# Weight residues, token sums and the first weight sums around the layer norms move from GpSimd to VectorE, the high copies of the plain slabs from VectorE to ScalarE

## The chip, the cores and the metric

The kernel runs on one core of a Trainium2 chip. The metric is the device time of one launch in microseconds (us), as the median of several runs. The five instruction streams of the core are called PE (TensorE), DVE (VectorE), ACT (ScalarE), POOL (GpSimd) and SP (SyncE, which here only issues DMAs).

## What is computed

An inference step of a two-layer streaming encoder over 576 tokens (512 of a prompt, 64 of a running stream), with D = 1024 and a hidden width of 4096. Layer 0 mixes tokens by chunked band attention, layer 1 by a Mamba-2 scan; each is followed by a dense MLP with squared ReLU. Around all four sublayers stands a post-norm residual. Cut to what matters here:

```python
def _layer_norm(x, g, b):
    mu = mean(x); var = mean(square(x - mu))
    return (x - mu) * rsqrt(var + 1e-5) * g + b

def _mlp(x, w_up, w_down):
    return square(relu(x @ w_up)) @ w_down

for i in range(2):
    m = attention(x) if i % 2 == 0 else ssm(x)
    x = _layer_norm(ALPHA * x + m, ln_mix_g[i], ln_mix_b[i])
    x = _layer_norm(ALPHA * x + _mlp(x, w_ff_up[i], w_ff_down[i]), ln_ff_g[i], ln_ff_b[i])
```

All of it is float32, and the outputs are the new x, the new attention caches and the scan's states.

## The kernel before

**Operands.** Activations lie transposed (features on partitions, tokens along the row) in `x32`, 8 blocks of 128 x 576. Each operand of a matmul is split into a high part (a copy rounded to the matmul's type: `wh` of a weight, `xh` of x, `hh` of a hidden tile, `th` of a sum of tokens) and a low residue, which is the value less that copy (`wl`, `xl`, `hl`, `tl`). A product is three matmuls: high by high, high by low, low by high (`dense`, L313; `dense_half`, L343; `product`, L546).

**Weights.** They come as slabs of 128 x 1024 in the order of `weight_plan`; a raw slab `wr` (four buffers) is loaded by SP, and `Weights.split` makes `wh` on ACT (L188) and `wl` (L189). Split pairs have five buffers, and one is given back when PE has used it (`drop`). L189 runs on DVE, except for the seven slabs around the head of each MLP and of the Mamba input projection (three before that head and four from it on: `pool_lo`, 21 slabs in all), for which it runs on POOL. The matmuls of an MLP's first layer are done in a Strassen form from its seventh slab on; the pair of raw slabs is then first added and subtracted in place in four pieces of 128 x 512 on POOL (L202, L204, L205, L210 in `produce`).

**A layer norm** is a generator that PE's issue loop steps (`side.tick`). It sums x over its blocks (L398 on POOL, in `resid`), has PE average that over the partitions (L406), subtracts (L410, DVE), squares (L413, ACT), adds the squares (L417, L418, DVE), has PE sum them (L367) and forms an inverse root on 96 x 3 values in a row of small DVE instructions (L371, L355, L357, then L360, L361, L362 three times; `y` is the result). PE spreads `y` (L377), DVE multiplies (L428), ACT applies gain and bias (L434), and copies and residues follow (`xh` L439 or L441, `xl` L442 on DVE). The norm is done in halves of 288 tokens. The first half runs beside the last matmuls of the sublayer ahead (`out_last`, the second half of its tokens), the second half beside the first matmuls of the sublayer behind (for an MLP `first_tiles`).

**The first tiles of an MLP.** Six tiles of the first layer are plain. Five of them are made in halves of the tokens (`dense_half`), the first halves beside the norm's second half. `act` then takes a tile out: Relu (L484) and Square (L485) on ACT, the high copy `hh` (L486) on DVE, the residue `hl` (L487) on DVE. Beside the second halves `combos` makes the sums of tokens that the Strassen products need: L502 and L511 on DVE, L506, L514, L515 and L519 on POOL, each with a copy on ACT (L490) and a residue on DVE (L491).

**Order.** Each engine runs its instructions in one fixed order, made when the kernel is built by a scheduler that places all engines' work together. An instruction whose operand isn't there yet holds up all that stand behind it on its engine.

Three stretches of the program are touched: the norm between attention and the first MLP (LN0 below, 300 to 395 us of the span), the norm between that MLP and the Mamba projection (LN1, 725 to 770 us) and the norm between the Mamba layer and the second MLP (LN2, 1240 to 1360 us).

Of the kernel before, what the change touches and what calls it, by code (L numbers as in the profile page):

```python
# [5 lines left out]
F32 = mybir.dt.float32  # L6
# [3 lines left out]
ALU = mybir.AluOpType  # L10
# [31 lines left out]
PLAIN = 6  # L42
DLAG = 5
HALFK = 512
LA = 4
PL0 = -3
PL1 = 4
WARM = 7
HE = 17
DE = 40  # L50
# [34 lines left out]
def weight_plan():  # L85
    plan = []
    for hp in range(8):
        plan += [("q", hp), ("k", hp), ("v", hp)]
    plan += [("wo", c, mp) for c in range(2) for mp in range(4)]

    def mlp(layer):
        p = [("up", layer, 0, m) for m in range(PLAIN)]
        for kind, q, i0, i1 in MLP_ORDER:
            if kind == "up":
                p += [("ups", layer, q, i, g) for i in range(i0, i1) for g in (2, 4, 1, 3)]
            else:
                p += [("down", layer, q, m) for m in range(8)]
        return p

    plan += mlp(0)  # L100
    for g in range(G):
        if g == 0:
            plan += [("dt",), ("c", g), ("b", g), ("x", 2 * g), ("x", 2 * g + 1), ("z", 0), ("z", 1)]
        else:
            plan += [(k, g if k in "cb" else 2 * g + j) for (k, j) in GORD]
        if g in (2, 4):
            plan += [("so", g // 2 - 1, mp) for mp in range(4)]
    plan += [("so", c, mp) for c in (2, 3) for mp in range(4)]
    plan += mlp(1)
    return plan  # L110


def build(nc, io):
    from contextlib import ExitStack
    plan = weight_plan()
    with tile.TileContext(nc) as tc, ExitStack() as es:
        V, S, PE, GP, SY = nc.vector, nc.scalar, nc.tensor, nc.gpsimd, nc.sync
# [9 lines left out]
        def tmp(w=NT):  # L127
            return tp.tile([P, w], F32, name="tmp", tag="tmp")
# [17 lines left out]
        x32 = xp.tile([P, 8, NT], F32, name="x32")  # L146
        xh = xp.tile([P, 8, NT], F32R, name="xh")
        xl = xp.tile([P, 8, NT], F32R, name="xl")

        heads_of = [i for i, p in enumerate(plan) if p[0] in ("up", "c") and p[1:] in ((0, 0, 0), (1, 0, 0), (0,))]  # L150
        pool_lo = {i + j for i in heads_of for j in range(PL0, PL1)}

        class Weights:
            def __init__(self):
                self.done = 0
# [24 lines left out]

            def split(self, i, *raws):
                hi, lo = self.alloc()
                eng = GP if i in pool_lo else V
                c = 0
                for raw in raws:
                    sl = slice(c, c + raw.shape[-1])
                    c = sl.stop
                    S.copy(hi[:, sl], raw)  # L188
                    eng.tensor_tensor(out=lo[:, sl], in0=raw, in1=hi[:, sl].bitcast(F32), op=ALU.subtract)  # L189
                self.t[i] = (hi, lo)  # L190

            def produce(self, i):
                p = plan[i]
                r = self.raw_free
                if p[0] != "ups":
                    self.split(i, self.raw.pop(r))
                    self.raw_free += 1
                    return
                r1, r2 = self.raw[r], self.raw[r + 1]
                lo, hi = slice(0, HALFK), slice(HALFK, 1024)  # L200
                if p[4] == 2:
                    GP.tensor_tensor(out=r2[:, lo], in0=r1[:, lo], in1=r2[:, lo], op=ALU.subtract)  # L202
                    self.split(i, r2)
                    GP.tensor_tensor(out=r2[:, hi], in0=r2[:, hi], in1=r2[:, lo], op=ALU.subtract)  # L204
                    GP.tensor_tensor(out=r2[:, lo], in0=r1[:, lo], in1=r2[:, hi], op=ALU.add)  # L205
                elif p[4] == 4:
                    self.split(i, r2[:, lo])
                elif p[4] == 1:
                    self.split(i, r1)
                    GP.tensor_tensor(out=r1[:, hi], in0=r1[:, hi], in1=r2[:, hi], op=ALU.subtract)  # L210
                else:
                    self.split(i, r2[:, hi], r1[:, hi])
                    del self.raw[r], self.raw[r + 1]
                    self.raw_free += 2
                    self.prefetch()
# [254 lines left out]
        def mlp(layer, ln_in, ln, final):  # L470
            with tc.tile_pool(name=f"mlp{layer}", bufs=1) as hpool:
# [3 lines left out]
                T1, T2 = slice(0, HALF), slice(HALF, NT)  # L475
# [5 lines left out]
                def act(src, q, m, t0, t1):  # L481
                    u, t = tmp(), tmp()
                    hh, hl = (x[:, m % 2, t0:t1] for x in H[q, m // 2])
                    S.activation(u[:, t0:t1], src, AF.Relu)  # L484
                    S.activation(t[:, t0:t1], u[:, t0:t1], AF.Square)  # L485
                    V.tensor_copy(hh, t[:, t0:t1])  # L486
                    V.tensor_tensor(out=hl, in0=t[:, t0:t1], in1=hh.bitcast(F32), op=ALU.subtract)  # L487

                def combine(dh, dl, t):
                    S.copy(dh, t)  # L490
                    V.tensor_tensor(out=dl, in0=t, in1=dh.bitcast(F32), op=ALU.subtract)  # L491

                def sums_of(kk):
                    t = tmp().rearrange("p (a b) -> p a b", a=2)
                    return t, slice(2 * kk, 2 * kk + 2), slice(4 + 2 * kk, 6 + 2 * kk)

                def combos():
                    k1, k2 = slice(0, 4), slice(4, 8)
                    for kk in range(2):
                        o = slice(2 * kk, 2 * kk + 2)  # L500
                        t, j1, j2 = sums_of(kk)
                        V.tensor_tensor(out=t, in0=x32[:, j2, T2], in1=x32[:, j1, T2], op=ALU.subtract)  # L502
                        combine(th[:, o, :], tl[:, o, :], t)
                        yield
                    t2 = collect()
                    GP.tensor_tensor(out=t2, in0=x32[:, k2, T2], in1=x32[:, k1, T2], op=ALU.subtract)  # L506
                    yield
                    for kk in range(2):
                        o1, o4 = slice(4 + 2 * kk, 6 + 2 * kk), slice(8 + 2 * kk, 10 + 2 * kk)
                        t, j1, j2 = sums_of(kk)  # L510
                        V.tensor_tensor(out=t, in0=x32[:, j1, T2], in1=x32[:, j1, T1], op=ALU.subtract)  # L511
                        combine(th[:, o1, :], tl[:, o1, :], t)
                        yield
                        GP.tensor_tensor(out=t, in0=t, in1=x32[:, j2, T2], op=ALU.subtract)  # L514
                        GP.tensor_tensor(out=t, in0=t, in1=x32[:, j2, T1], op=ALU.add)  # L515
                        yield
                        combine(th[:, o4, :], tl[:, o4, :], t)
                        yield
                    GP.tensor_tensor(out=t2, in0=t2, in1=x32[:, k1, T1], op=ALU.add)  # L519
                    last.append(t2)  # L520

                last = []
# [1 line left out]
                def collect():  # L524
                    return hpool.tile([P, 4, HALF], F32, name="ut", tag="ut", bufs=2)
# [361 lines left out]
        def ssm():  # L887
            cumd = dr.tile([32, NT], F32, name="cumd")
            expd = dr.tile([32, NT], F32, name="expd")
            with tc.tile_pool(name="ssm", bufs=2) as ap:  # L890
# [156 lines left out]
                def ssd(g, c, b, x0, x1, z0, z1):  # L1047
# [120 lines left out]
                    if g < 6:  # L1168
                        split(g, yy)
                    else:  # L1170
                        ys[g] = yy
# [20 lines left out]
                for g in (6, 7):  # L1192
                    split(g, ys[g])
# [79 lines left out]
def make(A):  # L1273
    import concourse.bacc as bacc
    nc = bacc.Bacc("TRN2", target_bir_lowering=False, num_devices=1)
    io = {}
    for k, a in A.items():
        io[k] = nc.dram_tensor("in_" + k, a.shape, F32, kind="ExternalInput").ap()
    for k, s in OUTS.items():
        io[k] = nc.dram_tensor("out_" + k, s, F32, kind="ExternalOutput").ap()  # L1280
    build(nc, io)
    return nc
# [20 lines left out]
```

## Time and profile before

| | before |
|---|---|
| median of 3 runs | 1732.73 us (1728.52 to 1733.08) |
| the profiled execution | 1731.92 us |
| its span | 1730.1 us |
| mean granted clock of PE | 0.981 of full speed |
| busy: PE, DVE, ACT, POOL | 1667.4, 1085.2, 767.3, 460.0 us |
| share of the chain that ended last: PE, DVE, ACT, POOL | 87%, 7%, 2%, 1% |

The span is the profiled execution from its first to its last instruction; some 1.8 us of the execution's time lie around it. Busy time is the sum over an engine's instructions, and two engines can be busy at once. The chain of work that ended last is followed back from the last instruction; an engine's share in it is the time that this engine's work, or what it waited for, sets directly. A granted clock below 1 means that in some stretches PE was run at the lower of its two speeds.

### The profile page before, as it was taken

The page shows a single profiled execution, that of the slowest core. Times are in us where ns is not written, and L with a number is a line of the kernel's source. Part 1 is how long each engine was busy: PE and PEld are TensorE (multiplying, and loading weights), DVE is VectorE, ACT ScalarE, POOL GpSimd, SP SyncE. Part 2 cuts the span into 40 slices and gives each one's busy share as a digit, 9 for nine tenths or more (in the row PEclk, how much of TensorE's full clock was granted, in tenths as well). Part 3 has the DMA queues.
Part 4 walks back from the last instruction along what each step waited for, and adds up shares of the span by engine and source line. Part 5 has one row for each costly group of instructions (what it writes and reads, how often), then busy time and mean ns, then how long its engine had stood idle before and what let it go on. Part 6 is the DMA issues. An engine that isn't in the chain of part 4 may idle for free.

```text
span 1730.1 us, 30824 instructions
## 1 busy us (share of the span) xinstructions
PE 1667.4 (96%) x12545; PEld 1591.5 (92%) x12545; DVE 1085.2 (63%) x1860; ACT 767.3 (44%) x1256; POOL 460.0 (27%) x453
## 2 busy tenths in 40 slices
PE   9999999889999999989999999999988999999995
PEld 8888887779999999989899999999978999999995
DVE  6555565795363736377876776777768836455446
ACT  5434442445261625245663563565225616254332
POOL 0000001441221212336541341344343313131211
PEclk9999999989999999999999999999998999999998
DMA  8343331103141323213332332333210312223121
GB/s 267 104 127 102 109 110 65 61 20 127 38 136 58 103 69 118 66 61 120 116 107 83 99 107 87 95 107 101 66 61 25 110 55 93 86 74 122 50 74 55
DMA packets 76925, 157.22 MB, mean 91 GB/s; under 512 B 11440, under 2 KB 40240, under 8 KB 76784
## 3 DMA queue, kind: packets, MB, share of 16 engines
q1 hardware_dynamic: 76784, 155.25, 27.7%
q8 instruction: 99, 1.62, 0.4%
q14 instruction: 42, 0.34, 0.1%
HBM read 145.80 MB, written 9.42 MB: 90 GB/s over the span
## 4 chain that ended last, share of the span: by engine, by line
PE 87%; DVE 7%; ACT 2%; POOL 1%; issue 1%; DMA 0%; SPq 0%; POOLq 0%; DVEq 0%; ACTq 0%
PE mm L313 54%; PE ax L546 12%; PE mm L546 5%; PE mm L343 2%; PE ax L802 2%; PE mm L322 1%; PE ax L824 1%; PE ax L1107 1%; PE ax L773 1%; PE ax L1110 1%; DVE tmp L417 1%; PE ax L377 1%; PE ax L1112 1%; PE ax L783 1%; PE ax L367 1%
## 5 line engine op out<-in xcount | busy, mean ns | idle before, releaser
L188 ACT CAST wh<-wr 128x1024 fp32r<-128x1024 f32 (+1 forms) x301 | 281.6, 938 | 476.4 <-PE mm L313 351.1
L189 DVE TENSOR_TENSOR wl<-wr,wh 128x1024 fp32r<-128x1024 f32 (+1 forms) x280 | 332.1, 1189 | 103.1 <-ACT wh L188 97.6
L313 PE MATMUL mm<-xh,wh 128*128 128x288 f32 x1088 | 239.9, 302 | 7.1 <-ACT tmp L484 7.0
L313 PE MATMUL mm<-xh,wl 128*128 128x288 f32 x1088 | 239.7, 301 | 0.0
L313 PE MATMUL mm<-xl,wh 128*128 128x288 f32 x1088 | 239.5, 301 | 0.0
L313 PE MATMUL mm<-hh,wl 128*128 128x288 f32 x960 | 223.4, 298 | 0.0
L313 PE MATMUL mm<-hh,wh 128*128 128x288 f32 x960 | 223.1, 298 | 0.0
L313 PE MATMUL mm<-hl,wh 128*128 128x288 f32 x960 | 222.9, 297 | 0.0
L389 DVE TENSOR_TENSOR x<-x,mm 128x288 f32<-128x288 f32 (+1 forms) x112 | 64.7, 581 | 206.8 <-PE mm L313 195.8
L313 PEld LDWEIGHTS mm<-xh,wh 128*128 128x128 f32 x1088 | 176.6, 191 | 9.9 <-ACT tmp L484 7.4
L313 PEld LDWEIGHTS mm<-xl,wh 128*128 128x128 f32 x1088 | 176.3, 191 | 4.1 <-issue 3.8
L313 PEld LDWEIGHTS mm<-xh,wl 128*128 128x128 f32 x1088 | 176.2, 190 | 1.5
L313 PEld LDWEIGHTS mm<-hh,wl 128*128 128x128 f32 x960 | 161.3, 190 | 0.1
L313 PEld LDWEIGHTS mm<-hl,wh 128*128 128x128 f32 x960 | 161.4, 190 | 0.0
L313 PEld LDWEIGHTS mm<-hh,wh 128*128 128x128 f32 x960 | 161.2, 190 | 0.1
L546 PE MATMUL ax<-xh,wh 128*128 128x288 f32 x416 | 122.9, 295 | 0.4 <-ACT ut L564 0.4
L546 PE MATMUL ax<-xl,wh 128*128 128x288 f32 x416 | 122.6, 295 | 0.0
L546 PE MATMUL ax<-xh,wl 128*128 128x288 f32 x416 | 122.5, 294 | 0.0
L202 POOL TENSOR_TENSOR wr<-wr 128x512 f32<-128x512 f32 x26 | 35.7, 1374 | 271.5 <-DMA wr<-in_wts 271.4
L918 DVE SCALAR_TENSOR_TENSOR tmp<-xpad,pm,tmp 128x579 f32<-128x579 f32 x90 | 88.9, 987 | 1.6 <-ACT tmp L916 0.8
L343 PE MATMUL mm<-xl,wh 128*128 128x288 f32 x240 | 74.3, 310 | 8.1 <-DVE xl L442 8.0
L546 PEld LDWEIGHTS ax<-xh,wh 128*128 128x128 f32 x416 | 78.1, 188 | 1.3 <-ACT ut L564 1.3
(264 smaller groups left out, 3643.0 us busy)
## 6 DMA issues: line engine op xcount, KB each, us to landing
wr<-in_wts SPq DMA_DIRECT2D x223, 512.0 KB, 3.4
cumb<-cumd SPq DMA_DIRECT2D x32, 256.0 KB, 3.7
e<-expd SPq DMA_DIRECT2D x48, 64.0 KB, 3.5
tb<-in_rel SPq DMA_DIRECT2D x16, 160.0 KB, 3.0
out_k<-tmp SPq DMA_DIRECT2D x8, 288.0 KB, 2.4
out_v<-tmp SPq DMA_DIRECT2D x8, 288.0 KB, 2.1
tb<-in_rel SPq DMA_DIRECT2D x16, 144.0 KB, 2.9
ts<-in_rel SPq DMA_DIRECT2D x16, 144.0 KB, 3.1
```

Source lines behind the costliest of these rows:

```text
L188: S.copy(hi[:, sl], raw)
L189: eng.tensor_tensor(out=lo[:, sl], in0=raw, in1=hi[:, sl].bitcast(F32), op=ALU.subtract)
L202: GP.tensor_tensor(out=r2[:, lo], in0=r1[:, lo], in1=r2[:, lo], op=ALU.subtract)
L313: PE.matmul(ps[:, o:o + HALF], w, a(k)[:, t0:t0 + HALF], start=first and i == 0, stop=last and i == 2)
L322: PE.matmul(ps[:, PS0 + t0:PS0 + t0 + HALF], w, a(k)[:, t0:t0 + HALF], start=k == 0 and i == 0, stop=k == 7 and i == 2)
L343: PE.matmul(o, a, b[:, k, h * HALF:(h + 1) * HALF], start=k == 0 and i == 0, stop=k == 7 and i == 2)
L367: PE.matmul(ps[0:96, j:j + 1], vv[:, 96 * j:96 * j + 96], scale_col, start=True, stop=True)
L377: PE.matmul(ps[:, 96 * j:96 * j + 96], y[:, j0 + j:j0 + j + 1].to_broadcast([96, 128]), ident[0:96, 0:96], start=True, stop=True)
L389: V.tensor_tensor(out=dst, in0=dst, in1=src, op=ALU.add)
L546: chain(PE.matmul(out, a, b, start=not more and k == 0 and i == 0, stop=k == 3 and i == 2, skip_group_check=True), k or i or name != "t3")
L802: PE.transpose(pp[:, 128 * k:128 * k + 128], s[:, 128 * k:128 * k + 128], ident)
L918: V.scalar_tensor_tensor(out=acc, in0=xr[:, k:k + 579], scalar=col(k), in1=acc, op0=ALU.mult, op1=ALU.add)
```

## The change

All L189 residues run on DVE, and the table `pool_lo` goes. In `combos` the four kinds of POOL sums (L506, L514, L515, L519) run on DVE. The four weight sums of the first Strassen pair of each MLP run on DVE, those of all other pairs stay on POOL. The high copies `hh` of the plain tiles (L486) run on ACT. The sums L398 of the norms stay on POOL.

Counted over the program, DVE gets from POOL 21 residues of 128 x 1024, 4 token sums of 128 x 1152, 8 token sums of 128 x 576 and 8 weight sums of 128 x 512; ACT gets from DVE 22 copies, 20 of 128 x 288 and 2 of 128 x 576.

```diff
@@ class Weights, split
-                eng = GP if i in pool_lo else V
...
                     S.copy(hi[:, sl], raw)
-                    eng.tensor_tensor(out=lo[:, sl], in0=raw, in1=hi[:, sl].bitcast(F32), op=ALU.subtract)
+                    V.tensor_tensor(out=lo[:, sl], in0=raw, in1=hi[:, sl].bitcast(F32), op=ALU.subtract)
@@ class Weights, produce
+                eng = V if p[2:4] == (0, PLAIN // 2) else GP
                 if p[4] == 2:
-                    GP.tensor_tensor(out=r2[:, lo], in0=r1[:, lo], in1=r2[:, lo], op=ALU.subtract)
+                    eng.tensor_tensor(out=r2[:, lo], in0=r1[:, lo], in1=r2[:, lo], op=ALU.subtract)
...
@@ mlp, act
-                    V.tensor_copy(hh, t[:, t0:t1])
+                    S.copy(hh, t[:, t0:t1])
                     V.tensor_tensor(out=hl, in0=t[:, t0:t1], in1=hh.bitcast(F32), op=ALU.subtract)
@@ mlp, combos
-                    GP.tensor_tensor(out=t2, in0=x32[:, k2, T2], in1=x32[:, k1, T2], op=ALU.subtract)
+                    V.tensor_tensor(out=t2, in0=x32[:, k2, T2], in1=x32[:, k1, T2], op=ALU.subtract)
...
-                        GP.tensor_tensor(out=t, in0=t, in1=x32[:, j2, T2], op=ALU.subtract)
-                        GP.tensor_tensor(out=t, in0=t, in1=x32[:, j2, T1], op=ALU.add)
+                        V.tensor_tensor(out=t, in0=t, in1=x32[:, j2, T2], op=ALU.subtract)
+                        V.tensor_tensor(out=t, in0=t, in1=x32[:, j2, T1], op=ALU.add)
...
-                    GP.tensor_tensor(out=t2, in0=t2, in1=x32[:, k1, T1], op=ALU.add)
+                    V.tensor_tensor(out=t2, in0=t2, in1=x32[:, k1, T1], op=ALU.add)
```

Line numbers in the changed kernel are lower by 5 to 6 behind `split` (L355 there is the first product of a root step, L360 of the kernel before), and the scheduler makes a new order on every engine. Two places of DVE's order in LN0 show it. The first is the inverse root of the norm's first half, from the row that takes PE's sums (`v`) to the one before the multiplication of x. Before:

```order
L371 TENSOR_SCALAR v<-ax_3897 96x3
L355 TENSOR_SCALAR w<-v 96x3
L357 TENSOR_SCALAR y<-w 96x3
L360 TENSOR_TENSOR w<-y 96x3
L361 SCALAR_TENSOR_TENSOR w<-w,v 96x3
L362 SCALAR_TENSOR_TENSOR y<-w,y 96x3
L360 TENSOR_TENSOR w<-y 96x3
L389 TENSOR_TENSOR x_78<-x_78,mm 128x288
L361 SCALAR_TENSOR_TENSOR w<-w,v 96x3
```

The same place in the changed kernel:

```order
L366 TENSOR_SCALAR v<-ax_3897 96x3
L183 TENSOR_TENSOR wl<-wr,wh 128x1024
L350 TENSOR_SCALAR w<-v 96x3
L384 TENSOR_TENSOR x_78<-x_78,mm 128x288
L352 TENSOR_SCALAR y<-w 96x3
L355 TENSOR_TENSOR w<-y 96x3
L183 TENSOR_TENSOR wl<-wr,wh 128x1024
L356 SCALAR_TENSOR_TENSOR w<-w,v 96x3
L384 TENSOR_TENSOR x_78<-x_78,mm 128x288
L357 SCALAR_TENSOR_TENSOR y<-w,y 96x3
```

Two residues of weights (L183 there) now stand inside the row of small instructions, a third stands just ahead of it among the sums of squares, and a fourth right behind it.

The second place is the end of the norm's second half, where the last residues `xl` of x are made beside the sums of tokens. Before:

```order
L442 TENSOR_TENSOR xl<-x_78,xh 128x2x288
L502 TENSOR_TENSOR tmp<-x_78 128x576
L442 TENSOR_TENSOR xl<-x_78,xh 128x2x288
L486 CAST hh<-tmp 128x288
L491 TENSOR_TENSOR tl<-tmp,th 128x576
```

In the changed kernel, where L501 and L514 are the two sums of 128 x 1152 that were L506 and L519 on POOL:

```order
L437 TENSOR_TENSOR xl<-x_78,xh 128x2x288
L501 TENSOR_TENSOR ut<-x_78 128x1152
L437 TENSOR_TENSOR xl<-x_78,xh 128x2x288
L482 TENSOR_TENSOR hl<-tmp,hh 128x288
L497 TENSOR_TENSOR tmp<-x_78 128x576 x2
L506 TENSOR_TENSOR tmp<-x_78 128x576
L486 TENSOR_TENSOR tl<-tmp,th 128x576
L514 TENSOR_TENSOR ut<-ut,x_78 128x1152
```

One of those sums now stands ahead of the last `xl`, in the place of a smaller one, and the copy `hh` is gone from between them.

## Rows read from the trace of the kernel before

**Rows 1.** Waits of PE in LN0: line waited for, us in total, times, longest.

```profile
PE mm L343 <- DVE xl L442: 3.9, 1, 3.9
PE ax L377 <- DVE y L362: 3.8, 1, 3.8
PE mm L313 <- ACT tmp L484: 3.8, 1, 3.8
PE ax L367 <- ACT tmp L485: 1.8, 1, 1.8
```

**Rows 2.** Waits of PE in LN1.

```profile
PE ax L367 <- DVE tmp L418: 3.0, 2, 2.3
...
PE ax L406 <- POOL tmp L398: 0.5, 1, 0.5
```

**Rows 3.** Waits of PE in LN2.

```profile
PE ax L377 <- DVE y L362: 4.3, 2, 3.8
PE mm L343 <- DVE xl L442: 4.1, 2, 4.0
PE mm L313 <- ACT tmp L484: 3.2, 1, 3.2
PE mm L313 <- DVE yl L1179: 1.8, 1, 1.8
```

**Rows 4.** Busy us (x count) of PE, PEld, DVE, ACT, POOL; clock; DMA share, GB/s.

```profile
300.00:395.00 95.00, 79.21 (x530) 76.94 (x529) 79.62 (x115) 41.62 (x72) 44.93 (x30) 0.89 0.13 45
412.00:464.00 52.00, 52.00 (x392) 52.00 (x391) 16.69 (x20) 12.04 (x13) 6.48 (x5) 1.00 0.22 75
```

**Rows 5.** The same view: nine stretches at the lower clock; the last line is their sum.

```profile
324.90:331.70 6.80, 5.89 (x25) 5.90 (x26) 4.96 (x10) 3.47 (x7) 2.17 (x3) 0.50 0.25 77
...
1263.50:1266.90 3.40, 3.40 (x16) 3.40 (x16) 0.91 (x2) 0.00 (x0) 0.80 (x1) 0.50 0.48 154
...
sum 51.20, PE 44.27 PEld 43.01 DVE 43.39 ACT 28.30 POOL 21.15; mean PE 4.92 PEld 4.78 DVE 4.82 ACT 3.14 POOL 2.35
```

**Rows 6.** Timeline of DVE in LN0: start, us, line, operation [idle before].

```profile
312.64 2.47 DVE L417 TENSOR_TENSOR tmp<-tmp 128x576 f32<-128x576 f32 x1
...
315.40 0.75 DVE L417 TENSOR_TENSOR tmp<-tmp 128x576 f32<-128x576 f32 x1
...
317.22 0.94 DVE L418 TENSOR_TENSOR tmp<-tmp 128x288 f32<-128x288 f32 x1
...
323.30 2.26 DVE L361 SCALAR_TENSOR_TENSOR w<-w,v 96x3 f32<-96x3 f32 x1
325.59 0.16 DVE L362 SCALAR_TENSOR_TENSOR y<-w,y 96x3 f32<-96x3 f32 x1
...
330.74 0.75 DVE L442 TENSOR_TENSOR xl<-x,xh 128x576 fp32r<-128x576 f32 x1
...
357.82 3.23 DVE L502 TENSOR_TENSOR tmp<-x 128x576 f32<-128x576 f32 x1
360.98 3.16 DVE L442 TENSOR_TENSOR xl<-x,xh 128x576 fp32r<-128x576 f32 x1
```

**Rows 7.** Timeline of POOL in LN0.

```profile
312.10 2.40 POOL L189 TENSOR_TENSOR wl<-wr,wh 128x1024 fp32r<-128x1024 f32 x1 [3.43 <-ACT wh L188]
...
323.20 2.34 POOL L189 TENSOR_TENSOR wl<-wr,wh 128x1024 fp32r<-128x1024 f32 x1
...
357.72 2.71 POOL L506 TENSOR_TENSOR ut<-x 128x1152 f32<-128x1152 f32 x1 [13.91 <-ACT x L434]
360.51 3.02 POOL L519 TENSOR_TENSOR ut<-ut,x 128x1152 f32<-128x1152 f32 x1
```

**Rows 8.** Timeline of ACT in LN0.

```profile
376.97 1.56 ACT L188 CAST wh<-wr 128x512 fp32r<-128x512 f32 x2 [2.24 <-POOL wr L205]
379.33 0.67 ACT L490 CAST th<-tmp 128x576 fp32r<-128x576 f32 x1 [0.79 <-DVE tmp L511]
```

**Rows 9.** The page's costliest groups: DVE's residues of weights (busy us, mean ns).

```profile
L189 DVE TENSOR_TENSOR wl<-wr,wh 128x1024 fp32r<-128x1024 f32 (+1 forms) x280 | 332.1, 1189 | 103.1 <-ACT wh L188 97.6
```

More of the change, by code (lines that the diff above doesn't have):

```diff
@@ L45 @@
 LA = 4
-PL0 = -3
-PL1 = 4
 WARM = 7
@@ L148, in build @@
         xl = xp.tile([P, 8, NT], F32R, name="xl")
-        heads_of = [i for i, p in enumerate(plan) if p[0] in ("up", "c") and p[1:] in ((0, 0, 0), (1, 0, 0), (0,))]
-        pool_lo = {i + j for i in heads_of for j in range(PL0, PL1)}
         class Weights:
@@ L200, in produce @@
                 lo, hi = slice(0, HALFK), slice(HALFK, 1024)
+                eng = V if p[2:4] == (0, PLAIN // 2) else GP
                 if p[4] == 2:
-                    GP.tensor_tensor(out=r2[:, lo], in0=r1[:, lo], in1=r2[:, lo], op=ALU.subtract)
+                    eng.tensor_tensor(out=r2[:, lo], in0=r1[:, lo], in1=r2[:, lo], op=ALU.subtract)
                     self.split(i, r2)
-                    GP.tensor_tensor(out=r2[:, hi], in0=r2[:, hi], in1=r2[:, lo], op=ALU.subtract)
-                    GP.tensor_tensor(out=r2[:, lo], in0=r1[:, lo], in1=r2[:, hi], op=ALU.add)
+                    eng.tensor_tensor(out=r2[:, hi], in0=r2[:, hi], in1=r2[:, lo], op=ALU.subtract)
+                    eng.tensor_tensor(out=r2[:, lo], in0=r1[:, lo], in1=r2[:, hi], op=ALU.add)
                 elif p[4] == 4:
@@ L209, in produce @@
                     self.split(i, r1)
-                    GP.tensor_tensor(out=r1[:, hi], in0=r1[:, hi], in1=r2[:, hi], op=ALU.subtract)
+                    eng.tensor_tensor(out=r1[:, hi], in0=r1[:, hi], in1=r2[:, hi], op=ALU.subtract)
                 else:
```

## The prediction

> **What bounds the kernel.** I read the waits of PE first, stretch by stretch. Away from the norms there is nothing to win: in 52 us of a down stage PE is busy for 52.00 us at full clock [rows 4]. In LN0 eight waits sum to 15.8 us, three of them of nearly 4 us [rows 1]; in LN1 three sum to 5.7 [rows 2]; in LN2 ten sum to 17.9 [rows 3]. Together PE stands still for 39.4 us. The busy table adds a second loss: the 95 us of LN0 ran at a mean granted clock of 0.89 [rows 4], and nine stretches in or right behind these waits show 0.50, that is 1.2 instead of 2.4 GHz [rows 5].
>
> What ends the waits is DVE for the most part, so DVE's timeline comes next, with POOL's beside it. The sum L417 took 2.47 us at 312.64 and 0.75 us three microseconds later; the 96 x 3 product L361 took 2.26 us at 323.30, where its neighbour of the same size took 0.16; L502 and L442, both of 128 x 576, took 3.23 and 3.16 us, where another L442 cost 0.75 at 330.74 [rows 6]. Each of these four lies beside a long POOL instruction that began 0.1 to 0.5 us before it: residues at 312.10 and 323.20, token sums at 357.72 and 360.51 [rows 7]. Each of the four ends 0.6 us behind the POOL row, or with it for the small one: POOL's end, and then its own work. So DVE waits inside its instruction until POOL is done, and the excess of the four is 1.7 + 2.1 + 2.5 + 2.4 = 8.7 us. The second of them lies inside the chain to `y`, for which PE waits 3.8 us; the last is the `xl` for which PE waits 3.9 us [rows 1].
>
> The Trainium skill, "SBUF — State Buffer", section on SBUF's two separate sides, says that a DVE operation with two operands in SBUF and a GpSimd operation exclude each other for the whole instruction. The four rows agree; that some may be late for another reason is a rival below.
>
> **The change, part by part.** *Work that moves.* At 1.19 us for a residue [rows 9] and 0.75 us for a two-operand 128 x 576 [rows 6], scaled with the size for the others (an estimate), DVE gets 21 x 1.19 = 25.0, 8 x 0.75 = 6.0, 4 x 1.50 = 6.0 and 8 x 0.67 = 5.3 us: 42.3 us, of which LN0 and LN2 get 17.0 each and LN1 8.3. From this go the 22 copies of `hh`, which I don't count.
>
> *What goes.* With the moved work POOL has in these stretches little left but the sums L398 and the later Strassen pairs. If the lengthening goes, so do the waits that it makes. In LN0:
> - `y`. DVE begins the first L417 at 312.64 as before. From there to the end of L418 the changed order has three L417, one L418, two evictions and one residue: 3 x 0.75 + 3 x 0.45 + 1.19, less some 0.08 for each by which rows overlap, 4.3 us: 316.9, against 318.2 now [rows 6]. Behind it come PE's sums (0.9 us with the hop) and, up to `y`, two residues, three evictions and twelve small rows: 2.4 + 1.1 + 12 x 0.19 = 5.8 us. So `y` is there at 323.6, against 325.75. PE has about 38 matmuls, 5 us, to do meanwhile, so the wait of 3.8 us becomes about 0.5.
> - PE now reaches the first plain tile at about 326.9. The first `xl` began 5.0 us behind `y` [rows 6] and takes 0.75, with a wait of 0.5 for an eviction between them that falls away: 328.8. **A new wait of 1.9 us** stands there; before, the long wait for `y` hid it.
> - The second half: the L485 wait of 1.8 us goes, because its Square stood behind late sums (L417) in the queues. The `xl` wait of 3.9 goes; the sum ahead of the last `xl` costs 1.3 to 1.5 us where the two long rows together cost 6.4.
> - The 3.8 us for L484 is ACT's queue: the Relu stands behind copies that waited for L205 on POOL and for L511 on DVE [rows 8]. Both come early when POOL's row of sums is gone. I keep 0.3.
> - Kept: three small waits, for L418, L389 and L387, with 1.9 together. With 0.5, 1.9 and 0.3 from above: 4.6 us of waits are left of 15.8.
>
> *The lower clock.* At full clock 392 matmuls take 52.00 us, 0.133 each [rows 4]. The nine stretches hold 186 matmuls (25 in the first) in 44.27 us of busy time [rows 5], so they cost 44.27 - 186 x 0.133 = 19.6 us more than at full clock: 7.2 in LN0 (67 matmuls in three stretches), 2.6 in LN1 (30 in two), 9.8 in LN2 (89 in four). The Trainium skill, "TensorE: Matmul & The Clock Gate", section Terms, prices a lowered clock at the whole lowered time by the lost share of pulses; by that rule it would be 51.2 / 2 = 25.6 us. The rows decide for 19.6, since PE idles in part of those stretches. A wait as short as the 1.8 us for L1179 [rows 3] was followed by 3.4 us at the lower clock, which cost 3.40 - 16 x 0.133 = 1.3 us [rows 5]; I charge that for each wait of 1.9 us or more that is left.
>
> *The sum.*
> - LN0: at most 15.8 + 7.2 = 23.0 us. Left: 4.6 + 1.3 = 5.9. Gain 17.1.
> - LN1: at most 5.7 + 2.6 = 8.3. Seven residues on DVE ahead of the first `xh` leave a wait of about 2.3, as long as the longest now [rows 2], with 1.3 of clock, and L406 keeps its 0.5 (POOL's L398 stays). Gain 4.2.
> - LN2: at most 17.9 + 9.8 = 27.7. The four waits of rows 3 go, 13.4 us (L1179's residue stood beside one on POOL). Left: 4.5, the new 1.9, 1.3 of clock. Gain 20.0.
>
> Together 41.3 us from the profiled 1731.92: 1690.6, and since the median lies 0.8 above that execution, **1691 us**. What had no row before is the copy `hh` on ACT: at most 0.67 us, a copy of twice the size [rows 8], 22 times 14.7 us in two stretches where ACT is busy for 42 of 95 us [rows 4]; it costs nothing at best (ACT idles beside it), and at worst keeps the waits for L484. I take nothing, since Relu, Square and copy now follow each other without a hop to DVE and back. A price that the four rows can't exclude is that of DVE's own two-operand work against the remaining L398: 0.5 to 2 us.
>
> **The rivals.**
> 1. *ACT's queue keeps PE waiting.* The copies make ACT's queue longer by up to 7 us a stretch, and it also holds Square, gain and bias, `xh` and `wh`. Then the 3.8 and 3.2 us for L484 stay [rows 1, 3], with the lower clock behind them (2.4 and 2.8 us, of the shares of LN0 and LN2 above): 12.2 us less gain, 1703. For: ACT ends 8.8 us of these waits already. Against: ACT waited there for POOL and DVE, not the other way round [rows 8].
> 2. *Residues hold up the roots.* Those among the small rows wait for `wh` from ACT, as the first residue on POOL did for part of 3.43 us [rows 7], and `wh` waits for PE to free a buffer. On POOL that held up nobody; on DVE the whole chain to `y` stands behind it. Then the waits for `y` stay at 3.8 in LN0 and LN2, with about 2.6 of clock each: 2 x (3.3 + 2.6) = 11.8 less, 1703. Both rivals together: 1715.
> 3. *Slower: DVE is full.* DVE is busy 79.6 of 95 us in LN0 [rows 4]. If its long rows are long for a reason of its own and not POOL's, 17.0 us are added to 15.4 idle ones, and the idle ones are waits for PE that can't be filled. Then the added 42.3 us push the chain directly: up to 1774, or, with half hidden, 1753. It decides as soon as the rows of 2 to 3 us don't shrink. For: the share; the changed order puts residues into the chain. Against: the L417 at 315.40 and the L442 at 330.74, with no long POOL row beside them, took 0.75 [rows 6]. The Trainium skill, "Perfetto Trace Analysis", section Optimizing Scalar/DVE Operations, advises to offload a saturated DVE, even to GPSIMD, with the reservation that the two share a port: the first half speaks against this change, and by it 1753 would be the time; the rows above go with the reservation.
> 4. *The waits were set elsewhere,* by PE's own order or by loads, and the change only renames them: 1732.
>
> **How the numbers follow.** The forecast as summed, within 10 us for the terms that a walk by hand misses (hops of 0.1 to 0.2 us between engines, a lower clock behind one wait more or less): 0.66. Rivals 1 or 2: 0.22, both at once included. More than the sum, to the floor of 1673 at which no wait and no lower clock is left: 0.03. No change: 0.05; slower: 0.04. The range from 1679 to 1712 holds the first and all of the second but its far end. What a measurement can tell from no change is 0.3%, 5.2 us: faster 0.91, within 0.05, slower 0.04.
>
> **What would show it.** Right: DVE's L417, L361, L502 and L442 rows (five lines lower in the changed code) take 0.75, 0.16, 0.75, 0.75 us everywhere in these stretches; the waits for `y` are under 1 us, that for `xl` is gone, a new one of about 2 us stands ahead of the first plain tile; PE's clock shows 0.50 in at most one short stretch for each norm; DVE's busy time rises by less than the 42 us, because what it no longer waits for is in that count too. Wrong in size: PE waits for L484 or `y` as long as before, with ACT or a `wh` copy ahead of it. Wrong in mechanism: DVE's rows stay at 2 to 3 us with POOL idle beside them.

## The result and the profile after

The changed kernel takes 1702.03 us (median of 4 runs, 1701.69 to 1706.24) against 1731.3 us before (4 runs): a ratio of 0.9838 with an interval of 0.9816 to 0.9860, so 24 to 32 us faster. The forecast of 1691 overstated the gain: 41 us were forecast, 30.2 came (spans 1730.1 and 1699.9 of the profiled executions). The range held it, but 1702 lies 11 us above the sum, outside the 10 us that the forecast gave to the sum itself. Two executions, one of e5 at 4016 us and one of the kernel before beside it at 2737 us, lie far off all others and are left out of the times and ratios below.

The page of the changed kernel, busy time of each engine:

```profile
PE 1652.7 (97%) x12545; PEld 1576.5 (93%) x12545; DVE 1064.4 (63%) x1879; ACT 774.8 (46%) x1278; POOL 378.1 (22%) x412
```

Two things stand in this line. PE's busy time fell by 14.7 us with the same 12545 matmuls: that is the lower clock. The other 15.5 us of the 30.2 are time in which PE stood still. And DVE's busy time fell by 20.8 us (1085.2 before) although it was given 41 instructions of POOL's, some 42 us of work by the prediction's prices, less the 22 copies (12.6 us before): what went is time in which its instructions stood still.

The busy table of three stretches that hold the norms in the changed kernel (busy us and count of PE, PEld, DVE, ACT, POOL, then the granted clock) answers to [rows 4]:

```profile
300.00:380.00 80.00, 74.72 (x538) 72.35 (x538) 67.21 (x118) 45.82 (x84) 17.21 (x14) 0.98 0.13 42
705.00:755.00 50.00, 45.10 (x322) 43.41 (x321) 36.15 (x70) 21.01 (x34) 8.38 (x16) 0.97 0.17 56
1225.00:1325.00 100.00, 90.98 (x668) 88.37 (x666) 79.33 (x145) 48.22 (x87) 21.44 (x17) 0.97 0.13 44
```

The clock of LN0 went from 0.89 in its 95 us to 0.98 in these 80. Of the nine stretches at the lower clock in and behind the norms [rows 5] three are left, one for each norm, 13.7 us where there were 51.2:

```profile
332.40:335.80 3.40, 3.40 (x14) 3.10 (x13) 2.59 (x4) 2.16 (x5) 1.09 (x1) 0.50 0.00 0
735.10:738.50 3.40, 3.29 (x12) 3.00 (x13) 3.40 (x5) 3.37 (x6) 0.06 (x1) 0.50 0.36 107
1277.80:1284.70 6.90, 3.87 (x15) 3.44 (x15) 6.78 (x11) 5.99 (x12) 0.00 (x0) 0.51 0.22 78
```

PE's waits in LN0, LN1 and LN2, one below the other, answer to [rows 1 to 3]:

```profile
PE mm L338 <- DVE x L384: 2.2, 1, 2.2
PE ax L372 <- DVE y L357: 1.1, 1, 1.1
PE mm L338 <- ACT tmp L479: 0.9, 1, 0.9
PE mm L308 <- DVE x L384: 0.7, 2, 0.4
PE mm L308 <- DVE x L382: 0.3, 1, 0.3
...
PE mm L338 <- DVE xh L434: 2.5, 1, 2.5
PE ax L362 <- DVE tmp L413: 0.9, 1, 0.9
PE ax L401 <- POOL tmp L393: 0.9, 1, 0.9
...
PE ax L401 <- POOL tmp L393: 2.7, 1, 2.7
PE mm L338 <- DVE xh L434: 2.5, 1, 2.5
PE mm L308 <- DVE x L384: 2.2, 3, 1.5
PE mm L541 <- ACT ut L552: 1.5, 1, 1.5
```

The three waits for `y`, `xl` and L484 that took 11.5 us in LN0 are 1.1, none and none; the 0.9 for L479 stands ahead of a half tile, where PE waited 0.7 for L484 before. New is the wait of 2.2 to 2.5 us ahead of the first plain tile (L338 for L384 or for `xh`), in every norm; and one that the prediction doesn't have, L541 for L552, in the Strassen products behind LN2 and, outside this window at 390 us, behind LN0.

How much each norm gave is read from PE landmarks: the first instruction of LN1's averages (L406, now L401), before and after, and the same statistics row of the Mamba stage (L367, now L362), before and after. The view is that of one source line in a window, with first and last start:

```profile
L406 PE MATMUL ax<-tmp,invd x2: 405/405/405, 726.6 to 726.9; 128*128 128x288 f32 x2
```

```profile
L401 PE MATMUL ax<-tmp,invd x2: 405/405/405, 713.1 to 713.4; 128*128 128x288 f32 x2
```

```profile
L367 PE MATMUL ax<-inv,tmp x12: 166/223/223, 1028.9 to 1029.8; 128*96 128x1 f32 x12
```

```profile
L362 PE MATMUL ax<-inv,tmp x12: 166/223/223, 1014.5 to 1015.4; 128*96 128x1 f32 x12
```

LN0 gave 726.6 - 713.1 = 13.5 us (17.1 forecast), LN1 14.4 - 13.5 = 0.9 (4.2 forecast), LN2 the rest, 30.2 - 14.4 = 15.8 (20.0 forecast).

DVE's timeline of LN0 in the changed kernel shows a part of why it was less than the walk by hand had it:

```profile
313.40 0.76 DVE L412 TENSOR_TENSOR tmp<-tmp 128x576 f32<-128x576 f32 x1
...
315.11 1.22 DVE L183 TENSOR_TENSOR wl<-wr,wh 128x1024 fp32r<-128x1024 f32 x1
...
318.64 1.71 DVE L183 TENSOR_TENSOR wl<-wr,wh 128x1024 fp32r<-128x1024 f32 x1
...
320.98 1.84 DVE L183 TENSOR_TENSOR wl<-wr,wh 128x1024 fp32r<-128x1024 f32 x1
...
323.55 0.67 DVE L356 SCALAR_TENSOR_TENSOR w<-w,v 96x3 f32<-96x3 f32 x1
...
325.07 0.65 DVE L357 SCALAR_TENSOR_TENSOR y<-w,y 96x3 f32<-96x3 f32 x1
```

The L412 rows take 0.76 us, as forecast. But the two residues inside the root take 1.71 and 1.84 instead of 1.22, and two of the 96 x 3 rows 0.67 and 0.65 instead of 0.16: 2.1 us in all. Beside each of them POOL runs one of the norm's sums, L393:

```profile
318.47 0.80 POOL L393 TENSOR_TENSOR tmp<-tmp,x 128x288 f32<-128x288 f32 x1
320.93 0.81 POOL L393 TENSOR_TENSOR tmp<-tmp,x 128x288 f32<-128x288 f32 x1 [1.66 <-DVE y L352]
323.39 0.81 POOL L393 TENSOR_TENSOR tmp<-tmp,x 128x288 f32<-128x288 f32 x1 [1.66 <-DVE y L357]
324.92 0.79 POOL L393 TENSOR_TENSOR tmp<-tmp,x 128x288 f32<-128x288 f32 x1 [0.72 <-DVE w L355]
...
367.18 5.95 POOL L197 TENSOR_TENSOR wr<-wr 128x512 f32<-128x512 f32 x1 [33.68 <-DMA wr<-in_wts]
```

The last row is the other way round: the first weight sum of the second Strassen pair, 1.30 us in the median of 24 such rows, stood on POOL for 5.95 us while DVE ran one two-operand row after the other. The wait of L541 comes from the second pair's sums on POOL, as e6 below shows; that this one row is what made them late is read from the rows and not tested.

So `y` is ready at 325.72 us, as late as before (325.75). Counted from PE's average it comes after 16.0 us instead of 16.8; in LN1 after 16.2 instead of 16.5, in LN2 after 17.1 instead of 17.5. The residues' own time and L393 take nearly all that the short rows give back. PE's wait for `y` fell all the same, because in the new order PE does more of the sublayer's matmuls (L308, before L313) between the average and the spread of `y`: 90 instead of 70 in LN0, 101 and 82 instead of 70 in LN1 and LN2. The busy table from the average to the spread in LN0, before and after:

```profile
308.93:325.81 16.88, 11.25 (x81) 10.23 (x79) 15.74 (x27) 5.45 (x7) 9.99 (x6) 0.97 0.17 63
309.69:325.78 16.09, 13.98 (x101) 12.93 (x99) 15.13 (x32) 6.50 (x8) 4.09 (x5) 1.00 0.29 99
```

PE is busy 2.7 us longer there, in a stretch that is 0.8 us shorter. The chain to the last `xl` of the second half did get shorter: from PE's average to the end of that row 28.1 us before and 23.2 after.

### The profile page after: what moved, and what is told of

The parts are those of the page before. It is cut to its first block, busy times and chain, and to the rows that moved or that the text cites. A ratio compares the mean times of both kernels' runs of the same rounds, so it can differ in the third digit from the quotient of the medians.

```text
span 1699.9 us, 30804 instructions
## 1 busy us (share of the span) xinstructions
PE 1652.7 (97%) x12545; PEld 1576.5 (93%) x12545; DVE 1064.4 (63%) x1879; ACT 774.8 (46%) x1278; POOL 378.1 (22%) x412
## 5 line engine op out<-in xcount | busy, mean ns | idle before, releaser
L183 DVE TENSOR_TENSOR wl<-wr,wh 128x1024 fp32r<-128x1024 f32 (+1 forms) x301 | 359.9, 1200 | 106.1 <-ACT wh L182 100.9
L308 PE MATMUL mm<-xh,wl 128*128 128x288 f32 x1088 | 237.8, 299 | 0.0
L308 PE MATMUL mm<-xh,wh 128*128 128x288 f32 x1088 | 237.5, 300 | 0.1
L308 PE MATMUL mm<-xl,wh 128*128 128x288 f32 x1088 | 237.4, 299 | 0.0
L308 PE MATMUL mm<-hh,wl 128*128 128x288 f32 x960 | 222.0, 297 | 0.0
L308 PE MATMUL mm<-hl,wh 128*128 128x288 f32 x960 | 221.7, 296 | 0.0
L308 PE MATMUL mm<-hh,wh 128*128 128x288 f32 x960 | 221.7, 296 | 0.0
L384 DVE TENSOR_TENSOR x<-x,mm 128x288 f32<-128x288 f32 (+1 forms) x112 | 64.5, 580 | 196.2 <-PE mm L308 185.1
L308 PEld LDWEIGHTS mm<-xl,wh 128*128 128x128 f32 x1088 | 174.3, 189 | 4.1 <-issue 3.8
L308 PEld LDWEIGHTS mm<-xh,wh 128*128 128x128 f32 x1088 | 174.5, 188 | 2.6 <-issue 1.4
L308 PEld LDWEIGHTS mm<-xh,wl 128*128 128x128 f32 x1088 | 174.3, 189 | 1.5
L308 PEld LDWEIGHTS mm<-hh,wl 128*128 128x128 f32 x960 | 160.1, 188 | 0.1
L308 PEld LDWEIGHTS mm<-hh,wh 128*128 128x128 f32 x960 | 160.1, 188 | 0.1
L308 PEld LDWEIGHTS mm<-hl,wh 128*128 128x128 f32 x960 | 160.1, 188 | 0.0
L541 PE MATMUL ax<-xh,wh 128*128 128x288 f32 x416 | 123.1, 296 | 0.5 <-ACT ut L559 0.4
L541 PE MATMUL ax<-xl,wh 128*128 128x288 f32 x416 | 122.6, 295 | 0.0
L541 PE MATMUL ax<-xh,wl 128*128 128x288 f32 x416 | 122.5, 294 | 0.0
L197 POOL TENSOR_TENSOR wr<-wr 128x512 f32<-128x512 f32 x24 | 40.7, 1695 | 337.9 <-DMA wr<-in_wts 297.8
L338 PE MATMUL mm<-xh,wh 128*128 128x288 f32 x240 | 72.8, 307 | 8.3 <-DVE xh L434 5.1
L541 PEld LDWEIGHTS ax<-xh,wh 128*128 128x128 f32 x416 | 78.1, 188 | 1.6 <-ACT ut L559 1.3
```

Of the source, the lines that this page charges most:

```text
L183: V.tensor_tensor(out=lo[:, sl], in0=raw, in1=hi[:, sl].bitcast(F32), op=ALU.subtract)
L197: eng.tensor_tensor(out=r2[:, lo], in0=r1[:, lo], in1=r2[:, lo], op=ALU.subtract)
L308: PE.matmul(ps[:, o:o + HALF], w, a(k)[:, t0:t0 + HALF], start=first and i == 0, stop=last and i == 2)
L338: PE.matmul(o, a, b[:, k, h * HALF:(h + 1) * HALF], start=k == 0 and i == 0, stop=k == 7 and i == 2)
L384: V.tensor_tensor(out=dst, in0=dst, in1=src, op=ALU.add)
L541: chain(PE.matmul(out, a, b, start=not more and k == 0 and i == 0, stop=k == 3 and i == 2, skip_group_check=True), k or i or name != "t3")
```

## The experiments

Theory A: a two-operand row of DVE stands still while a POOL row runs, and those made the waits. Theory B: DVE is full, and more work on it costs time. Others stand with the runs. Each time is a median; the ratio is to the kernel before on the same chip.

| run | what | us | ratio, 95% |
|---|---|---|---|
| e1 | residues alone | 1721.73 | 0.9946 (0.9929 to 0.9964) |
| e2 | token and first weight sums alone | 1715.64 | 0.9908 (0.9884 to 0.9932) |
| e3 | copies `hh` alone | 1727.91 | 0.9979 (0.9968 to 0.9990) |
| e4 | the change without the residues | 1715.57 | 0.9902 (0.9875 to 0.9930) |
| e8 | the change with an idle twin of each residue on POOL | 1726.42 | 0.9971 (0.9957 to 0.9985) |
| e9 | the same with a twin of 128 x 8 | 1703.68 | 0.9832 (0.9818 to 0.9847) |
| e5 | the change, norm sums on DVE too | 1701.63 | 0.9821 (0.9796 to 0.9847) |
| e6 | the change, second pair's sums on DVE too | 1698.95 | 0.9813 (0.9792 to 0.9835) |
| e7 | e5 and e6 together | 1695.63 | 0.9795 (0.9772 to 0.9818) |
| e10 | e7, first `xh` on ACT | 1698.24 | 0.9797 (0.9782 to 0.9811) |
| e11 | e7, LN1's residues on POOL | 1696.68 | 0.9796 (0.9776 to 0.9815) |

**The parts alone.** e1 is the kernel before with

```diff
-                eng = GP if i in pool_lo else V
+                eng = V
```

> Kernel before with one part of the change: all 21 weight residues on VectorE; token sums, first weight sums and hh copies stay where they were. Theory A (VectorE's two-operand rows stand still while a GpSimd row runs, and that made the waits): L417 and L361 beside the norms fall to 0.75 and 0.2 us, the wait for y falls below 1.5 us in LN0 and LN2, the xl wait (3.9) and the L484 wait (3.8) stay; about 1717 us, 14 less than before. Theory B (VectorE is full, more work on it costs): the residues stand in the chain to y; not faster than before, 1731 or more.

It took 10.8 us less than before. In LN0 the wait for `y` is 1.1, those for `xl` and L484 stay:

```profile
PE mm L343 <- DVE xl L442: 4.1, 2, 4.0
PE mm L313 <- ACT tmp L484: 3.2, 1, 3.2
PE mm L343 <- DVE x L389: 2.2, 1, 2.2
PE ax L377 <- DVE y L362: 1.1, 1, 1.1
```

L417 fell to 0.76 us and L361 to between 0.15 and 0.67, as theory A has it, and 25 us more work on DVE made the kernel faster, against B. But `y` comes 16.0 us behind PE's average, as in the whole change, and PE has its 90 matmuls before the spread here too. A kernel with the residues on POOL and PE's later spread was not run, so how much of this gain is the order's and how much the short rows' isn't shown. The expectation left out the wait of 2.2 us ahead of the first plain tile, which is here as in the whole change; the gain is 3 us smaller than expected.

e2 moves the other POOL rows:

```diff
-                    GP.tensor_tensor(out=t2, in0=x32[:, k2, T2], in1=x32[:, k1, T2], op=ALU.subtract)
+                    V.tensor_tensor(out=t2, in0=x32[:, k2, T2], in1=x32[:, k1, T2], op=ALU.subtract)
...
+                eng = V if p[2:4] == (0, PLAIN // 2) else GP
```

> Kernel before with another part: token sums and the first pair's weight sums on VectorE; residues stay on GpSimd, hh copies on VectorE. Theory A: the xl wait (3.9 and 4.0) and the L484 wait (3.8 and 3.2) go with the lower clock behind them, the wait for y (3.8 and 3.8) stays; about 1714 us, 17 less than before. Theory B: 17 us of added VectorE work in LN0 and LN2 end up in front of the first Strassen products; 1731 or more.

It took 16.9 us less; in LN0 the wait for `y` is 3.8 as before, `xl` is gone, and a wait of 2.4 us for a weight residue (L189) stands where L484 stood. The last `xl` ends 22.9 us behind the average instead of 28.1. Theory A again, and here the chain itself is shorter.

e3 moves the copies alone:

```diff
-                    V.tensor_copy(hh, t[:, t0:t1])
+                    S.copy(hh, t[:, t0:t1])
```

> Kernel before with the last part alone: the 22 copies hh on ScalarE. Theory A: no wait is removed, since none of them was made by these copies; within 3 us of before (1728 to 1734). Theory C (the copies' hop between ScalarE and VectorE is what kept PE waiting for L484): the two L484 waits go, 10 us or more less than before, 1721.

It took 4.6 us less, a little more than theory A allowed by the medians (the interval, 0.9968 to 0.9990, allows 2 to 6 us). Theory C falls: the L484 wait didn't go but grew, in LN2 from 3.2 to 6.0 too. Theory A's "no wait is removed" isn't borne out either, for `xl` fell from 3.9 to 1.0. The waits of LN0 sum to 15.4 us, as good as before (15.8); what was won is for the most part the lower clock, since PE's busy time fell by 5.8 us to 1661.6:

```profile
PE mm L313 <- ACT tmp L484: 6.0, 1, 6.0
PE ax L377 <- DVE y L362: 3.8, 1, 3.8
PE ax L367 <- DVE tmp L418: 2.5, 2, 1.9
PE mm L343 <- DVE xl L442: 1.0, 1, 1.0
```

The three parts add up to 32 us, the whole change gave 29 by the medians: little of one is hidden by another. e4 is the check from the other side, the change with `pool_lo` kept.

> Changed kernel with the 21 weight residues back on GpSimd. Theory A: the gain splits by place, so this loses what the residues alone won: waits for y of 2 us or more in LN0 and LN2 and in LN1 as before; about 1716, 14 more than the changed kernel. Theory B: the residues on VectorE cost something, so taking them off gives 1702 or less.

It lost 13.5 us by the medians and 11 by the ratios, with the wait for `y` at 3.8 us in LN0, 3.5 in LN1 and 2.3 in LN2, about what theory A expected. PE is back at 70 matmuls before the spread, so this run doesn't part the order from the short rows either.

**The lock by itself.** These runs keep all the work of the change on DVE and ACT, and give POOL rows on which nothing depends but the raw slab's release:

```diff
+                if i in pool_lo:
+                    GP.tensor_tensor(out=raws[0], in0=raws[0], in1=hi.bitcast(F32), op=ALU.subtract)
                 self.t[i] = (hi, lo)
```

> Changed kernel, with GpSimd computing each of the 21 residues a second time, behind VectorE's own, into the raw slab that nobody reads any more. No result depends on it; VectorE and ScalarE have the work of the changed kernel. Theory A: VectorE's rows beside these twins take 2 to 3 us again (L412, L356, L437), the waits for y come back to 2 us or more; 1712 to 1722 us, 10 to 20 more than the changed kernel. Theory D (what counted was that nobody waits for GpSimd's results any more, not the lock): 1702 within 3.

It took 1726.42 us: 24 of the 29 us are lost again, more than the 10 to 20 of theory A. DVE's rows in LN0 (line numbers are those of the kernel before, the twin is L188):

```profile
316.90 2.24 DVE L418 TENSOR_TENSOR tmp<-tmp 128x288 f32<-128x288 f32 x1
...
322.78 0.45 DVE L389 TENSOR_TENSOR x<-x,mm 128x288 f32<-128x288 f32 x1 [0.95 <-PE mm L313]
323.15 1.09 DVE L357 TENSOR_SCALAR y<-w 96x3 int32<-96x3 int32 x1
...
326.48 2.13 DVE L362 SCALAR_TENSOR_TENSOR y<-w,y 96x3 f32<-96x3 f32 x1
```

and POOL's twins beside them:

```profile
316.08 2.74 POOL L188 TENSOR_TENSOR wr<-wr,wh 128x1024 f32<-128x1024 f32 x1 [7.03 <-ACT wh L185]
...
321.83 2.39 POOL L188 TENSOR_TENSOR wr<-wr,wh 128x1024 f32<-128x1024 f32 x1 [1.16 <-DVE w L355]
...
326.20 2.38 POOL L188 TENSOR_TENSOR wr<-wr,wh 128x1024 f32<-128x1024 f32 x1 [1.23 <-DVE w L361]
```

L418 takes 2.24 us instead of 0.45 and ends 0.32 behind the twin (318.82); the root's L362 takes 2.13 instead of 0.16 and ends with its twin (328.6). PE waits 2.7 us for `y` in LN0 and 4.8 in LN1; in LN2 it doesn't, the time lost there stands in other waits. DVE's busy time is 1082.6 us, 18 more than in the changed kernel, for the same DVE work.

The control shrinks the twin and keeps its waits, what it releases and its place in the program:

```diff
-                    GP.tensor_tensor(out=raws[0], in0=raws[0], in1=hi.bitcast(F32), op=ALU.subtract)
+                    GP.tensor_tensor(out=raws[0][:, 0:8], in0=raws[0][:, 0:8], in1=hi[:, 0:8].bitcast(F32), op=ALU.subtract)
```

> As the twin before (the changed kernel with a second residue on GpSimd that nobody reads), but of 128 x 8 elements instead of 128 x 1024: the same 21 instructions with the same waits and releases, and almost no time on GpSimd. Theory A (VectorE stands still while a GpSimd row runs): the time goes back to that of the changed kernel, 1702 within 4. Theory E (the twin cost time through its semaphores, the scheduler's other order or the later release of the raw slab): 1715 or more, as with the full twin.

It took 1703.68 us: the gain is back. Theory D falls with e8, and the semaphores and the order of theory E with e9: PE, DVE and ACT run the same instructions in the same order in the changed kernel, e8 and e9. The control doesn't hold the time of the slab's release, which the full twin puts off by its own length. If later slabs were the cause, DVE would idle more; outside its busy time the span has 640.0 us in e8 and 638.0 in e9, 2 of the 20.7 us by which the spans differ. The rest is longer rows: 22 of DVE's 1879 instructions take over 0.15 us more in e8, 24.4 us together, and inside each of them a POOL row ends. So it is the time that POOL's rows run.

**What was left.** e5 moves the norm's own sums too:

```diff
-POOL_S = 8
+POOL_S = 1
```

> Changed kernel with the norms' own sums (L393 there, 56 additions of 128 x 288) on VectorE too. Theory A: the rows that are still long beside them (0.65 to 1.84 us instead of 0.16 to 1.2) become normal and the waits for L393 (0.9, 2.7 and 1.5 us) go; 1694 to 1699. Theory B: 56 x 0.37 = 21 us more on VectorE, part of it in the chain to y; 1702 to 1710.

Inconclusive: 1701.63 us, the changed kernel's time. The waits for L393 are gone, but a wait for `y` of 2.4 us stands in LN2; the added rows may cost about what the lengthening had cost, but the run doesn't separate the two.

e6 moves the second pair's weight sums:

```diff
-                eng = V if p[2:4] == (0, PLAIN // 2) else GP
+                eng = V if p[2:4] in ((0, PLAIN // 2), (1, 0)) else GP
```

> Changed kernel with the weight sums of the second Strassen pair of each MLP on VectorE as well. In the changed kernel the first of them (L197) took 5.95 us on GpSimd beside VectorE's rows, where it takes 1.3, and PE waited 1.5 us for a drain behind it in both MLPs. Theory A: these two waits go; 1699, 3 less. Theory B: the same work on VectorE delays the first pair; 1702 or more.

It took 1698.95 us, 3.1 less than the changed kernel, as theory A has it, though the intervals of the two ratios overlap. L197 is now a DVE row of 0.68 us, and PE's wait of L541 is gone behind both norms. e7 takes both edits.

> Changed kernel with both: norm sums and the second pair's weight sums on VectorE. Theory A: the gains of both add, 1692 to 1697. Theory B: VectorE is full in the stretches around the norms, 1702 or more.

1695.63 us is the shortest median of the study, 6.4 us under the changed kernel's; the intervals of the two ratios just touch. What stays in it is a wait of 2.4 us for `y` in LN2 and, in all three norms, the wait ahead of the first plain tile. In LN0:

```profile
PE mm L338 <- DVE xh L434: 2.5, 1, 2.5
PE mm L338 <- ACT tmp L479: 1.1, 1, 1.1
PE mm L338 <- DVE xl L437: 0.5, 1, 0.5
```

e10 tried that wait (`XCP = 2` to `XCP = 0`).

> The kernel with norm sums and second pair on VectorE, and the first high copy of x in each norm half (L434) on ScalarE instead of VectorE. What is left there is a wait of 2.4 to 2.6 us for that copy in each of the three norms. If the copy's place in VectorE's queue makes that wait: 1690 to 1693. If the chain from y on is simply longer than PE's work beside it: 1695 within 2, the wait renamed to xl.

The ratio is that of e7 (0.9797 and 0.9795). The wait took another name and grew, in LN0 and in LN1 (in LN2 it fell from 2.4 to 2.1):

```profile
PE mm L338 <- ACT xh L436: 3.1, 1, 3.1
```

So taking the copy out of DVE's queue doesn't remove the wait. That the chain from `y` to the first `xh` is longer than PE's work beside it fits this; but the copy takes 0.65 us on ACT and 0.45 on DVE, so the run isn't a clean test of the copy's place. e11 puts LN1's seven residues back on POOL, in e7.

> The kernel with norm sums and second pair on VectorE, but with the seven residues around LN1 back on GpSimd. In LN1 the change won 0.9 us where 4.2 were forecast. If the residues in VectorE's chain cost there nearly what the standing still had cost: 1695 within 3. If they did win and something else ate it: 1698 or more.

The ratio is again e7's. In LN1 PE waits 3.5 us for L417 (the last sum of squares), 1.1 for `xh`, 0.9 for `xl` and 0.7 for `y`, 6.2 in all, where e7 has 2.6 for `xh`, 0.8 for `xl` and 0.6 for `y`, 4.0. So the residues in DVE's chain cost there nearly what the standing still had cost, to within some 2 us that the times can't separate.

## Why the prediction was right, and where its sum was too large

**The mechanism** of the long rows held. They fall to their short times where POOL is quiet, and the twin of e8 brings them back with no result depending on it. The Trainium skill, "SBUF — State Buffer", section on SBUF's two separate sides, says that a DVE operation with two operands in SBUF and a GpSimd operation exclude each other for the whole instruction; e8's L418 and L362, which end 0.32 us behind the twin and with it, agree. Of the signs named, the `xl` wait of LN0, the new wait of about 2 us, the lower clock in one stretch for each norm and DVE's busy time came as forecast; the wait for `y` in LN0 was 1.1 and not under 1, and two 96 x 3 rows took 0.65 and 0.67 us.

**The chain to `y`** didn't do what the prediction had it do. It put `y` at 323.6 instead of 325.75 us; `y` came at 325.72. That the wait still fell, from 3.8 to 1.1 us, is the 20 matmuls that PE has more before the spread. The prediction counted PE's work in the new order rightly (about 38 matmuls behind its sums), but put the gain down to DVE's shorter rows alone. So the time is within the range with this step wrong.

**The lower clock** was sized well: 19.6 less 3.9 us forecast, a gain of 15.7. By the prediction's own working the three stretches left cost 10.56 - 41 x 0.133 = 5.1 us, a gain of 14.5, and PE's busy time fell by 14.7.

**The waits** were not. The prediction's three stages leave 4.6, 2.8 and 6.4 us, 13.8 together, a gain of 25.6. PE's idle time fell by 15.5. In the lists of PE's waits 6.7 (with the 1.5 behind LN0), 5.1 and 10.4 us are left, 22.2 together. The mis-sized terms:
- "With the moved work POOL has in these stretches little left": the second pair's weight sums were left, and the first of them was held up by DVE's new rows. Two waits of 1.5 us; e6 removes them and 3.1 us.
- The price for L398, "0.5 to 2 us", was named but not put into the sum. It is 2.1 us in LN0's root alone, and PE's waits for L398 itself (now L393) grew from 0.7 to 2.7 in LN2 and from 0.5 to 0.9 in LN1. Going over to DVE doesn't win it back by itself (e5).
- The start: DVE's first L412 stood at 313.40, not at 312.64, since PE does the average of LN0 0.8 us later in its new order. "As before" was an assumption that the order could have corrected. These 0.8 us and the 2.1 of L393 are more than the 2.1 us by which `y` came later than forecast; other rows were shorter than the walk had them.
- The wait ahead of the first plain tile: 1.9, 2.3 and 1.9 us forecast, 2.2, 2.5 and 2.5 measured. The size was right, but in LN0 both of its ends were 2 us late (PE free at 328.8 and the tile at 331.1, forecast 326.9 and 328.8), so the late `y` cancels in it.
- LN1, 0.9 for 4.2: residues ahead of the first `xh` took 1.2 to 1.8 us each instead of 1.19, and e11 shows no gain from them that is clear of noise.

**The rivals.** ACT's queue (rival 1): not in the changed kernel, where the waits for L479 are 0.9 us; in e3, with the sums still on POOL, the copies on ACT did lengthen the waits for L484 to 6.0 us, though the kernel got faster. Residues that hold up the root (rival 2): true for the time of `y`, not through a wait for `wh`, for none of them idled, but through their own time and L393; PE's order hid most of it. The 1703 us that rivals 1 and 2 named lie next to the measured time, but the loss stands in other terms than theirs, so that is chance. DVE is full (rival 3): no; e1 and e2 put 25 and 17 us on it and gained 11 and 17. Renaming (rival 4): no, PE's waits and its time at the lower clock both fell.

## What to carry over

Before work is moved to GpSimd to relieve VectorE, look at VectorE's rows beside GpSimd's: a row two or three times as long as the same row elsewhere, ending with GpSimd's row, is a price that the busy shares hide, because standing still counts as busy. In the serial small-row chains of a norm, on which the matmuls wait, such a row costs its whole lengthening and then some time at the lower clock. Check also when the awaited result is ready, and not only how long PE waits for it: `y` was no earlier here, and its wait shrank because PE had other work. And when a chain is shortened, walk on to the next one: here it was the chain to the first tile and the next Strassen pair.

## What the runs showed that was not expected

GpSimd stands still too: a sum of 128 x 512 took 5.95 us instead of 1.30 beside a series of two-operand VectorE instructions (the profile's spans of POOL are rough).

Not every VectorE row is held up. In e8 the eviction L389, with one operand in PSUM, took its usual 0.45 us at 322.78 in the middle of a twin, while L357, a 96 x 3 row with a single operand in SBUF, right behind it took 1.09 and ended with the twin. In LN1 the same L357 took 2.30 us beside a twin of 2.38:

```profile
734.06 2.30 DVE L357 TENSOR_SCALAR y<-w 96x3 int32<-96x3 int32 x1
```

```profile
733.96 2.38 POOL L188 TENSOR_TENSOR wr<-wr,wh 128x1024 f32<-128x1024 f32 x1
```

A copy of 128 x 576 with a single operand (`xh`, L439) took 0.87 us in e8 instead of 0.45 and ended 0.32 us behind its twin. So in these runs small rows are no safer than large ones, and a single operand in SBUF is no protection.
